# The low parts of an ordinary weight block, made by one subtraction into two places of a ring of five

## The chip, the cores and the metric

The kernel runs on one core of one Trainium2 chip. The metric is device time in microseconds (us) of one launch. Of the kernel before there are three runs and one profiled execution with its trace.

## What is computed

The reference is a decoder trunk of two layers over 256 tokens of width 2048, all float32. Layer 0 mixes tokens by retention, layer 1 by a short gated convolution; each is followed by a SwiGLU feed-forward network (FFN). Cut to what carries the time:

```python
for i in range(2):
    mod = c_act @ w_mod[i] + b_mod[i]; sh1, sc1, g1, sh2, sc2, g2 = split(mod, 6)
    h = rms_norm(x, norm1_g[i]) * (1 + sc1) + sh1
    y = retention_mixer(h, ...) if i == 0 else short_conv_mixer(h, ...)   # h @ w_in ... @ w_out
    x = x + g1 * y
    h = rms_norm(x, norm2_g[i]) * (1 + sc2) + sh2
    a, b = split(h @ ffn_w_in[i], 2)
    x = x + g2 * ((silu(a) * b) @ ffn_w_out[i])
return rms_norm(x, final_g)
```

## The kernel before, in words

**High and low parts.** A float32 product is made of faster matmuls on values of type float32r. Each factor is split: the high part is the value cast to float32r (ScalarE), the low part is the value less its high part (VectorE). A product then takes three terms: high by high, high by low, low by high.

**The stream of weights.** All weights of the trunk's products stand in one array `w_all`, in blocks of 128 x 2048 (1 MB), in the order of use. A block lands in one of four `raw` buffers (`fetch`, L378). `prepare` (L393) then makes a piece of it ready: a cast on ScalarE (L419, named hi) and a subtraction on VectorE (L422, named lo). The parts go to a ring of `PLACES` = 5 places of 1024 columns each, one ring for the high and one for the low parts (L426). The list `pieces` (L376) says which pieces a block is cut into:

- an ordinary block is two pieces, (0, 1): its left and its right half, each with one cast and one subtraction of 1024 columns and one place;
- a block of class `Seven` (L134) serves a product of 2 x 2 blocks in seven multiplications instead of eight. It is four pieces, (2, 3, 4, 5): VectorE makes differences of the block's parts (L406, L410, L412), and the pieces take three places of 1024 columns and one place that holds only 512.

A piece numbered 6, a whole block into two places at once, is known to `prepare` and to `fits` (L431) but stands in no list of the kernel before.

**What sets the order.** TensorE's instructions run in the order in which the program is written. `take` (L434) hands the next weight columns to a matmul. When a place is used up, it is dropped, and behind the opening `take` calls `prepare` as long as `fits` allows: one place must be free for a piece, two for piece 6. So a place is written anew when TensorE has done with it, and TensorE comes to it again after the four other places. Behind the opening the instructions of VectorE and ScalarE are put in order by a scheduler, not by hand; each engine then runs its own list strictly in order. In the opening (the retention mixer's first input products) they stand in written order, and only one to three pieces are made ahead.

**How long a place lasts.** In `product` (L462: retention and convolution) a place of 1024 columns serves eight pairs of matmuls, of 512 and of 256 columns (L472, L475). In `by_token` (L492: the FFNs) an ordinary place serves twelve matmuls of 512 columns through `thrice` (L482 to L489, the rows of the trace being L485, L486 and L487; L486 is the one that reads the low part of the weights when they stream, and it comes second). A place of a Seven serves six of them (L201, `sevens`), its last place of 512 columns three.

**Which blocks are Sevens.** In each FFN the blocks of a group of columns come in rows of eight to twelve; the numbers of the rows that are Sevens are written down: `FFN_SEVEN` = (2, 4, 6) for the first FFN's input products (ten groups), `IN_SEVEN` = (3, 4, 6) for the last FFN's (ten groups), and `OUT_SEVEN` for its output products.

**Beside it on VectorE:** 192 modulation sums over blocks of 2048 columns (L326 and, in the opening, L798), sums and splits of results, and the mixers' own arithmetic.

Of the kernel before, what the change touches and what calls it, by code (L numbers as in the profile page):

```python
# [10 lines left out]
F32 = mybir.dt.float32  # L11
F32R = mybir.dt.float32r
I32 = mybir.dt.int32
AF = mybir.ActivationFunctionType
ALU = mybir.AluOpType
PSUM = bass.MemoryType.PSUM

P = 128
# [13 lines left out]
CHUNK = 2048  # L32
HALF = 1024
# [20 lines left out]
PLACES = 5  # L54
FETCHED, PLAIN, WARM, ADDED = 2, 3, (5, 0, 0, 0, 0, 0, 0, 8), ()
# [23 lines left out]
def ret_in_groups():  # L79

    qkg, v = [], []
    for h in range(HEADS):
        q = [Q0 + h * DK + i * P for i in range(2)]
        k = [K0 + h * DK + i * P for i in range(2)]
        qkg.append([q, k, [(G0 + h * DV, DV)]])
        v.append(Group([V0 + h * DV], DV))
    done = [0] * HEADS  # L90
    spans = []
    for heads, (a, b) in SPANS:
        assert all(done[h] == a for h in heads)
        for h in heads:
            done[h] = b
        spans.append(Group([c for h in heads for part in qkg[h] for c in part], ks=range(a, b)))
    rest = [[Group(c, ks=range(done[h], KT)) for c in qkg[h]] for h in range(HEADS)]
    return spans, list(zip(rest, v))
# [28 lines left out]
RET_SPANS, RET_HEADS = ret_in_groups()  # L127
# [6 lines left out]
class Seven:  # L134
# [6 lines left out]
    n = 2 * DV // P  # L141
# [123 lines left out]
def trunk(ctx: ExitStack, tc: tile.TileContext, x_in, c_in, pos_in, w_mod, cols_in, gain_in, tab_in, w_all, out):  # L265
    nc = tc.nc
    const = ctx.enter_context(tc.tile_pool(name="const", bufs=1))
    work = ctx.enter_context(tc.tile_pool(name="work", bufs=2))
    wpool = ctx.enter_context(tc.tile_pool(name="wpool", bufs=1))
# [8 lines left out]
    def tmp(tag, shape=(P, S), dtype=F32, pool=work, bufs=None):  # L278
        return pool.tile(list(shape), dtype, tag=tag, name=name(tag), bufs=bufs)
# [12 lines left out]
    at = [0]  # L292
# [76 lines left out]
    ready, place, raws, fetched, n_fetched = [], [None], [], {}, [0]  # L369
    in_seven, n = set(), 0  # L370
# [2 lines left out]
            in_seven.add(n // CHUNK)  # L373
        n += g.n * P * len(g.ks)

    pieces = [(i, p) for i in range(PLAIN, w_all.shape[0]) for p in ((2, 3, 4, 5) if i in in_seven else (0, 1))]  # L376

    def fetch():  # L378
        raw = wpool.tile([P, CHUNK], F32, tag="raw", name=name("raw"), bufs=RAW_BUFS)
        nc.sync.dma_start(raw, w_all[n_fetched[0]])  # L380
        fetched[n_fetched[0]] = raw
        n_fetched[0] += 1
# [3 lines left out]
    def next_raw(i=None):  # L386
        i = used[0] if i is None else i
        used[0] += i < PLAIN
        while n_fetched[0] <= i + (FETCHED if i < PLAIN else 0):
            fetch()  # L390
        return fetched.pop(i)

    def prepare(between=None):  # L393
        if prepared[0] == len(pieces):
            return
        index, piece = pieces[prepared[0]]
        prepared[0] += 1
        if piece in (0, 2, 6):
            raws[:] = [next_raw(index)]
            while first <= units[0] < early and len(fetched) < RAW_BUFS - 1 and n_fetched[0] < w_all.shape[0]:  # L400
                fetch()
        whole = raws[0]
        b = [whole[:, i : i + DV] for i in range(0, CHUNK, DV)]
        raw = whole[:, :HALF] if piece in (0, 4) else whole[:, HALF:] if piece < 6 else whole
        if piece == 2:
            nc.vector.tensor_tensor(differences[0], whole[:, DV : 3 * DV], whole[:, : 2 * DV], op=ALU.subtract)  # L406
        elif piece == 3:
            raw = differences[0]
        elif piece == 4:
            nc.vector.tensor_tensor(b[1], b[2], differences[0][:, :DV], op=ALU.subtract)  # L410
        elif piece == 5:
            nc.vector.tensor_tensor(b[3], b[3], b[1], op=ALU.subtract)  # L412
            raw = b[3]
        width, at = raw.shape[1], HALF * (taken_places[0] % PLACES)
        taken_places[0] += -(-width // HALF)
        hi, lo = [t[:, at : at + width] for t in split_weights]
        steps = [slice(i, min(i + HALF, width)) for i in range(0, width, HALF)]
        for o in steps:
            nc.scalar.copy(hi[:, o], raw[:, o])  # L419
        if between:  # L420
            between()
        nc.vector.tensor_tensor(lo, raw, hi.bitcast(F32), op=ALU.subtract)  # L422
        ready.extend((hi[:, o], lo[:, o], o.stop - o.start) for o in steps)

    taken_places = [0]
    split_weights = [  # L426
        wpool.tile([P, PLACES * HALF], F32R, tag=tag, name=tag) for tag in ("hi", "lo")
    ]
    prepared = [0]

# [3 lines left out]
    def take(group, k, col, width=P):  # L434

        assert order.pop() == (group, k, col, width)
        i = place[0] or 0
        if i == 0:
            if place[0] == 0:
                ready.pop(0)  # L440
            while len(ready) < 1 + AHEAD * (units[0] >= first) or units[0] >= early and fits():
                n = len(ready)
                prepare()
                if len(ready) == n:
                    break
        place[0] = (i + width) % ready[0][2]
        return [t[:, i : i + width] for t in ready[0][:2]]
# [274 lines left out]
    with ExitStack() as inner:  # L722
# [64 lines left out]
        with tc.tile_pool(name="start", bufs=1) as sp:  # L787
# [59 lines left out]
            with tc.manual_schedule(engines={mybir.EngineType.DVE, mybir.EngineType.Activation}):  # L847
# [92 lines left out]
                def between(k):  # L940
                    lows[k]()
                    both_reduced(k)
                    if k == FIRST_KS - 1 and PLAIN == FIRST_KS:
                        prepare()
                        prepare()
# [10 lines left out]
            due, step = [], [0.0]  # L956
            at, plain_rows = 0.0, range(PLAIN - FIRST_KS)
            if plain_rows:
                due += [(len(plain_rows) - PREPARED + 0.5 * i, prepare) for i in range(2)]
            for k in range(FIRST_KS, KT):  # L960
                steps = ROW_STEPS[(k >= ROWS_AT[0]) + (k >= ROWS_AT[1])]
# [358 lines left out]
    with tc.tile_pool(name="ffn", bufs=1) as fpool:  # L1320
# [5 lines left out]
        for part in range(2):  # L1326
            n = FFN_TILES[part] // 2
# [19 lines left out]
    for i, g in enumerate(CONV_IN):  # L1347
        pending += [sums(g)] if i else normed(acc, 1, 0, g)
        while len(pending) >= 3:
# [3 lines left out]
            b, c, u = pb(tmp("bsum", pool=mpool, bufs=2)), pc(), pu()  # L1353
# [149 lines left out]
    for part in range(2):  # L1503
        n = LAST_TILES[part] // 2
# [54 lines left out]
```

## Time and profile before

| | before |
|---|---|
| three runs, median (lowest, highest) | 2562.66 us (2562.12, 2562.8) |
| the profiled execution's span, first to last instruction | 2558.4 us, 4.3 us less than the median run |
| TensorE (PE) busy | 2539.3 us, 99% |
| VectorE (DVE) busy | 2354.7 us, 92% |
| ScalarE (ACT) busy | 1351.2 us, 53% |
| DMA, mean | 269 GB/s |

The profiled execution has no time of its own beside its span; what lies around the span is taken as the 4.3 us. In the rows a start is in us from the span's start, and after it comes the duration; "x3" is three instructions in a row merged into one. PE is a matmul, PEld its weight load. A matmul's end is modelled, and matmuls overlap, so the distance of two starts says how long TensorE really takes for one.

### The profile page before, as it was taken

How to read it: one execution, taken by the hardware profiler on the slowest of the kernel's cores; microseconds unless marked ns; L12 is line 12 of the kernel's file. 1: busy time of each engine (PE TensorE's matmuls, PEld its weight loads, DVE VectorE, ACT ScalarE, POOL GpSimd, SP SyncE). 2: the span in 40 equal slices, each digit the busy share in tenths (PEclk: the TensorE clock that was granted, in tenths of full speed). 3: DMA queues.
4: the chain of work that ended last, by engine and by line, in shares of the span. 5: the costliest groups of instructions: out<-in, count | busy, mean ns of one | idle time of the engine just before them, and what ended most of it. 6: DMA issues, size and time to landing. Idle time of an engine off the chain costs nothing.

```text
span 2558.4 us, 34761 instructions
## 1 busy us (share of the span) xinstructions
PE 2539.3 (99%) x13237; PEld 2181.4 (85%) x13237; DVE 2354.7 (92%) x2968; ACT 1351.2 (53%) x1799; POOL 179.3 (7%) x234
## 2 busy tenths in 40 slices
PE   8999999999999999999999999999999999999998
PEld 7898888888889888888888898888998888888886
DVE  7989999898899999889999899888989999999998
ACT  5544543454456554345555454445566555555554
POOL 0000121011110001000000012000000000000001
PEclk9999999999999999999999999999999999999999
DMA  9987888879875667866667879888846465555653
GB/s 399 396 329 264 319 317 340 333 287 331 325 281 213 237 234 293 336 249 228 216 228 299 328 270 344 314 306 309 323 158 215 180 230 214 181 214 183 228 183 146
DMA packets 96695, 689.47 MB, mean 269 GB/s; under 512 B 10744, under 2 KB 12168, under 8 KB 13456
## 3 DMA queue, kind: packets, MB, share of 16 engines
q1 hardware_dynamic: 96528, 687.25, 72.2%
q8 instruction: 103, 1.69, 0.3%
q14 instruction: 64, 0.52, 0.1%
HBM read 685.11 MB, written 2.11 MB: 269 GB/s over the span
## 4 chain that ended last, share of the span: by engine, by line
PE 94%; DVE 3%; DMA 1%; ACT 1%; issue 1%; POOL 0%; SPq 0%; ACTq 0%; POOLq 0%; DVEq 0%
PE bank L472 22%; PE bank L487 17%; PE bank L485 17%; PE bank L486 17%; PE bank L475 11%; DVE lo L422 1%; PE bank L667 1%; PE bank L669 1%; PE bank L668 1%; PE bank L536 1%; PE bank L535 1%; PE bank L534 1%; DVE raw L798 1%; DMA raw<-w_all 1%; PE bank L1290 1%; PE bank L1067 1%
## 5 line engine op out<-in xcount | busy, mean ns | idle before, releaser
L419 ACT CAST hi<-raw 128x1024 fp32r<-128x1024 f32 (+1 forms) x984 | 991.1, 1019 | 936.7 <-PE bank L487 325.1
L422 DVE TENSOR_TENSOR lo<-raw,hi 128x1024 fp32r<-128x1024 f32 (+1 forms) x984 | 1143.3, 1179 | 125.6 <-ACT hi L419 116.7
L485 PE MATMUL bank<-hi,h 128*128 128x512 f32 x1540 | 602.9, 391 | 0.0
L487 PE MATMUL bank<-hi,h 128*128 128x512 f32 x1540 | 601.2, 390 | 0.0
L486 PE MATMUL bank<-lo,h 128*128 128x512 f32 x1540 | 601.1, 390 | 0.0
L326 DVE SCALAR_TENSOR_TENSOR raw<-raw,cb 128x2048 f32<-128x2048 f32 x160 | 365.4, 2285 | 8.2 <-DMA raw<-w_mod 8.0
L472 PE MATMUL bank<-h,hi 128*128 128x512 f32 x1012 | 352.8, 392 | 0.0
L487 PEld LDWEIGHTS bank<-hi,h 128*128 128x128 f32 x1540 | 289.4, 188 | 61.0
L485 PEld LDWEIGHTS bank<-hi,h 128*128 128x128 f32 x1540 | 289.6, 188 | 58.1
L486 PEld LDWEIGHTS bank<-lo,h 128*128 128x128 f32 x1540 | 289.7, 188 | 57.5
L472 PE MATMUL bank<-mid,hi 128*128 128x512 f32 x920 | 319.4, 391 | 0.0
L475 PE MATMUL bank<-h,lo 128*128 128x256 f32 x1012 | 285.0, 282 | 0.0
L475 PE MATMUL bank<-mid,lo 128*128 128x256 f32 x920 | 259.7, 282 | 0.0
L472 PEld LDWEIGHTS bank<-h,hi 128*128 128x128 f32 x1012 | 190.1, 188 | 40.3
L472 PEld LDWEIGHTS bank<-mid,hi 128*128 128x128 f32 x920 | 172.9, 188 | 35.6
L475 PEld LDWEIGHTS bank<-h,lo 128*128 128x128 f32 x1012 | 191.6, 189 | 0.5
L475 PEld LDWEIGHTS bank<-mid,lo 128*128 128x128 f32 x920 | 174.3, 189 | 0.1
L472 PE MATMUL bank<-rm,hi 128*128 128x512 f32 x496 | 172.5, 391 | 0.0
L475 PE MATMUL bank<-rm,lo 128*128 128x256 f32 x496 | 140.0, 282 | 0.0
L487 PE MATMUL bank<-hi,mid 128*128 128x512 f32 x284 | 110.9, 391 | 0.0
L485 PE MATMUL bank<-hi,mid 128*128 128x512 f32 x284 | 110.9, 391 | 0.0
L486 PE MATMUL bank<-lo,mid 128*128 128x512 f32 x284 | 110.7, 390 | 0.0
(300 smaller groups left out, 3344.2 us busy)
## 6 DMA issues: line engine op xcount, KB each, us to landing
raw<-w_all SPq DMA_DIRECT2D x456, 1024.0 KB, 5.0
raw<-w_mod SPq DMA_DIRECT2D x192, 1024.0 KB, 6.1
x<-x_in SPq DMA_DIRECT2D x4, 512.0 KB, 5.3
out<-xt SPq DMA_DIRECT2D x4, 512.0 KB, 3.0
decay<-tab_in SPq DMA_DIRECT2D x8, 128.0 KB, 4.9
x<-gate_row SPq DMA_DIRECT2D x2, 512.0 KB, 4.6
last_gain<-gain_in SPq DMA_DIRECT2D x1, 1024.0 KB
cols<-cols_in SPq DMA_DIRECT2D x1, 152.0 KB, 8.2
```

The source lines that it names most:

```text
L326: nc.vector.scalar_tensor_tensor(raw, raw, 1.0, cb, op0=ALU.mult, op1=ALU.mult, accum_out=total)
L419: nc.scalar.copy(hi[:, o], raw[:, o])
L422: nc.vector.tensor_tensor(lo, raw, hi.bitcast(F32), op=ALU.subtract)
L472: nc.tensor.matmul(pt, hi, h, start=fresh and k == g.ks[0], stop=False, skip_group_check=True)
L475: nc.tensor.matmul(pt[:, 1, :], lo, h[:, 0, :], start=False, stop=last and k == g.ks[-1], skip_group_check=True)
L485: nc.tensor.matmul(o, hi, w_hi, start=first, stop=False)
L486: nc.tensor.matmul(o, hi, w_lo, start=False, stop=False)
L487: nc.tensor.matmul(o, lo, w_hi, start=False, stop=last)
L534: nc.tensor.matmul(pt, hi, h[:, 0, :], start=first, stop=False, skip_group_check=True)
L535: nc.tensor.matmul(pt, hi, h[:, 1, :], start=False, stop=False, skip_group_check=True)
L536: nc.tensor.matmul(pt, lo, h[:, 0, :], start=False, stop=last, skip_group_check=True)
L667: nc.tensor.matmul(pt, hi, high, start=k == 0, stop=False, skip_group_check=True)
```

## The change

An ordinary block behind the opening (`apart` lists the blocks of the opening) becomes one piece, number 6. Its two casts stay two instructions of 1024 columns; its two subtractions become one of 2048 columns, which writes two places of the ring at once. The ring tile gets a dimension for the place, so that the two places may also be the last and the first (a step of -4 places). Since piece 6 needs two free places, `take` asks for an ordinary block when the second of two places has been used up. Blocks of the opening and Sevens keep their pieces.

```diff
-    pieces = [(i, p) for i in range(PLAIN, w_all.shape[0]) for p in ((2, 3, 4, 5) if i in in_seven else (0, 1))]
+    apart = range(sum(g.n * len(g.ks) for g in RET_SPANS) * P // CHUNK + 1)
+    pieces = [(i, p) for i in range(PLAIN, w_all.shape[0]) for p in ((2, 3, 4, 5) if i in in_seven else (0, 1) if i in apart else (6,))]
...
-        width, at = raw.shape[1], HALF * (taken_places[0] % PLACES)
-        taken_places[0] += -(-width // HALF)
-        hi, lo = [t[:, at : at + width] for t in split_weights]
-        steps = [slice(i, min(i + HALF, width)) for i in range(0, width, HALF)]
-        for o in steps:
-            nc.scalar.copy(hi[:, o], raw[:, o])
+        width, at = raw.shape[1], taken_places[0] % PLACES
+        n = -(-width // HALF)
+        taken_places[0] += n
+        rows = [raw[:, i : min(i + HALF, width)] for i in range(0, width, HALF)]
+        his, los = [[t[:, (at + i) % PLACES, : v.shape[1]] for i, v in enumerate(rows)] for t in split_weights]
+        for hi, v in zip(his, rows):
+            nc.scalar.copy(hi, v)
         if between:
             between()
-        nc.vector.tensor_tensor(lo, raw, hi.bitcast(F32), op=ALU.subtract)
-        ready.extend((hi[:, o], lo[:, o], o.stop - o.start) for o in steps)
+        if n == 1:
+            nc.vector.tensor_tensor(los[0], raw, his[0].bitcast(F32), op=ALU.subtract)
+        else:
+            step = 1 if at + 1 < PLACES else 1 - PLACES
+            end = None if at + 2 * step < 0 else at + 2 * step
+            hi, lo = [t[:, at:end:step, :] for t in split_weights]
+            raw = raw.rearrange("p (a b) -> p a b", a=2)
+            nc.vector.tensor_tensor(lo, raw, hi.bitcast(F32), op=ALU.subtract)
+        ready.extend((hi, lo, v.shape[1]) for hi, lo, v in zip(his, los, rows))
...
-        wpool.tile([P, PLACES * HALF], F32R, tag=tag, name=tag) for tag in ("hi", "lo")
+        wpool.tile([P, PLACES, HALF], F32R, tag=tag, name=tag) for tag in ("hi", "lo")
```

Behind the opening 346 blocks become such pairs. Two places on VectorE show how its list changes. The first is in the last FFN. Here x8 is the tile of a Seven's differences, raw_2116 is a block of a Seven and raw_2115 the ordinary block used before it; the row that makes raw_2115's low parts comes behind the low parts of the Seven ahead of both (raw_2114, whose piece of 512 columns is the first row shown). Before:

```order
L422 TENSOR_TENSOR lo_94<-raw_2114_18769,hi_93 128x512
L406 TENSOR_TENSOR x8_75<-raw_2116_18821 128x1024
L422 TENSOR_TENSOR lo_94<-raw_2115_18803,hi_93 128x1024 x2
L422 TENSOR_TENSOR lo_94<-raw_2116_18821,hi_93 128x1024
L422 TENSOR_TENSOR lo_94<-x8_75,hi_93 128x1024
L410 TENSOR_TENSOR raw_2116_18821<-raw_2116_18821,x8_75 128x512
```

And now, with the rows of raw_2114 from its first low part on:

```order
L425 TENSOR_TENSOR lo_94<-raw_2114_18460,hi_93 128x1024
L413 TENSOR_TENSOR raw_2114_18460<-raw_2114_18460 128x512
L425 TENSOR_TENSOR lo_94<-x8_75,hi_93 128x1024
L425 TENSOR_TENSOR lo_94<-raw_2114_18460,hi_93 128x1024
L425 TENSOR_TENSOR lo_94<-raw_2114_18460,hi_93 128x512
L407 TENSOR_TENSOR x8_75<-raw_2116_18511 128x1024
L411 TENSOR_TENSOR raw_2116_18511<-raw_2116_18511,x8_75 128x512
L431 TENSOR_TENSOR lo_94<-raw_2115_18500,hi_93 128x2048
L425 TENSOR_TENSOR lo_94<-raw_2116_18511,hi_93 128x1024
```

The two subtractions of raw_2115 have become one, and one more of the next Seven's differences (L411, before L410) now stands ahead of it.

The second place is in the convolution, where every block is ordinary. L326 is a modulation sum; sum, cu and y are tiles of the mixer. Before:

```order
L422 TENSOR_TENSOR lo_94<-raw_1608_13847,hi_93 128x1024
L326 SCALAR_TENSOR_TENSOR raw_1621_13939,msum_1622_13941<-raw_1621_13939,cb_71 128x2048
L546 TENSOR_TENSOR sum_1616_13900<-bank_1607_13846,low_1615_13898 128x256
L422 TENSOR_TENSOR lo_94<-raw_1620_13913,hi_93 128x1024
L1356 TENSOR_TENSOR cu_1617_13902<-sum_1614_13896,sum_1616_13900 128x256
L422 TENSOR_TENSOR lo_94<-raw_1620_13913,hi_93 128x1024
```

And now:

```order
L431 TENSOR_TENSOR lo_94<-raw_1610_13642,hi_93 128x2048
L326 SCALAR_TENSOR_TENSOR raw_1621_13711,msum_1622_13713<-raw_1621_13711,cb_71 128x2048
L555 TENSOR_TENSOR sum_1616_13673<-bank_1607_13620,low_1615_13671 128x256
L1365 TENSOR_TENSOR cu_1617_13675<-sum_1614_13669,sum_1616_13673 128x256
L431 TENSOR_TENSOR lo_94<-raw_1620_13702,hi_93 128x2048
```

The two halves of raw_1620 stood on both sides of the mixer's cu and are now one instruction behind it. TensorE's list has the same matmuls in the same order as before.

## The prediction

> **What bounds the kernel now.** I read the page's busy shares first, then the windows by stage, then the waits of TensorE behind the opening.
>
> ```profile
> span 2558.4 us, 34761 instructions
> PE 2539.3 (99%) x13237; PEld 2181.4 (85%) x13237; DVE 2354.7 (92%) x2968; ACT 1351.2 (53%) x1799; POOL 179.3 (7%) x234
> ```
>
> ```profile
> core 0: us, PE busy (x) PEld busy (x) DVE busy (x) ACT busy (x) POOL busy (x), PEclk, DMA share, GB/s
> 192.00:832.00 640.00, 639.46 (x3449) 554.55 (x3448) 590.09 (x802) 315.44 (x466) 83.27 (x109) 1.00 0.81 301
> 832.00:1360.00 528.00, 528.00 (x2514) 443.25 (x2513) 493.43 (x548) 279.42 (x306) 30.57 (x33) 1.00 0.69 253
> 1910.00:2558.00 648.00, 638.88 (x2854) 528.75 (x2852) 609.95 (x742) 372.59 (x445) 9.62 (x10) 1.00 0.55 197
> ```
>
> ```profile
> engine line waited for: us in total, times, longest us
> PE bank L1067 <- DVE sp L552: 0.5, 1, 0.5
> ```
>
> The last answer is that of TensorE's waits from 192 us, where the opening ends, up to 2540 us: one wait of 0.5 us. In the first FFN (832 to 1360) PE is busy without a gap, at the full clock. VectorE, though busy 93% there and 94% in the last FFN (1910 to 2558), holds nobody up. A share of 99% alone would not prove it, since a matmul's record overlaps the next one's; the starts do:
>
> ```profile
> 2234.01 0.39 PE L487 MATMUL bank<-hi,h 128*128 128x512 f32 x1
> 2234.24 0.39 PE L485 MATMUL bank<-hi,sum 128*128 128x512 f32 x1
> 2234.47 0.39 PE L486 MATMUL bank<-lo,sum 128*128 128x512 f32 x1
> ...
> 2237.64 0.39 PE L485 MATMUL bank<-hi,h 128*128 128x512 f32 x1
> 2237.87 0.39 PE L486 MATMUL bank<-lo,h 128*128 128x512 f32 x1
> ```
>
> From 2234.01 to 2237.87 there are 17 steps, 0.227 us each, the same 0.23 between neighbours: no gap. [...] So a gain on VectorE has next to nothing to shorten, and the question is whether the new form makes TensorE wait.
>
> **What is removed: 346 subtractions' starts.** The rows are the groups of VectorE by shape.
>
> ```profile
> L422 DVE TENSOR_TENSOR lo<-raw,hi 128x1024 fp32r<-128x1024 f32 x906 | 1096.0, 1221 | 124.8 <-ACT hi L419 115.9 <-PE bank L472 2.5
> L326 DVE SCALAR_TENSOR_TENSOR raw<-raw,cb 128x2048 f32<-128x2048 f32 x160 | 365.4, 2285 | 8.2 <-DMA raw<-w_mod 8.0
> ```
>
> A subtraction of 2048 isn't in the trace. One of 1024 takes 1.22; the nearest row with 2048 columns is the modulation sum, 2.29. I take 2.29 (upper end 2 x 1.22 = 2.44). Back to back, three of 1024 take 3.49 (row at 2235.32 below), that is (3.49 - 1.22) / 2 = 1.14 for each further one. A pair now takes 1.14 + 1.22 = 2.36, so 0.07 is saved, 346 times: 24 us of VectorE's time. As TensorE waits for VectorE behind the opening 0.5 us in all, I put that at 0. [...]
>
> **What is added: the first place of a pair waits for its second.** Before, the low part of the first half could be made as soon as its own place was free and cast. Now it must wait until TensorE has left the second place too, the second cast is done, and the double subtraction has run whole. Behind it on VectorE stand the next low parts and differences, and TensorE waits for it. When the second place comes free, TensorE has the three other places left to work on. How long these last decides.
>
> *Pairs among ordinary blocks.* In the convolution a place comes free at the end of the first row's matmul, and the pair that is then prepared is wanted by the second row:
>
> ```profile
> 1649.12 0.28 PE L475 MATMUL bank<-h,lo 128*128 128x256 f32 x1
> ...
> 1657.78 0.28 PE L475 MATMUL bank<-h,lo 128*128 128x256 f32 x1
> ```
>
> 1657.78 - 1649.40 = 8.38 us. The work to be done in it is 3.6 (below), so 4.8 is left, enough for two modulation sums of 2.29 in the way. I put these at 0. If that cover went, each would cost what its queue exceeds 4.8 by.
>
> *Pairs behind a Seven.* Here the three places are those of a Seven, 6 + 6 + 3 = 15 matmuls of 0.227, 3.4 us. By the written lists there are 30 in the first FFN (ten groups, rows 3, 5, 7) and 37 in the last (20 behind `IN_SEVEN`, rows 5 and 7 of ten groups; 17 in the outputs): 67. Take the place whose order is shown above. Its second place is left by the matmul at 2234.01, which ends at 2234.40; its low part is wanted at 2237.87: 3.47 us. Now the steps, from ScalarE and VectorE around there:
>
> ```profile
> 2228.36 1.05 ACT L419 CAST hi<-raw 128x1024 fp32r<-128x1024 f32 x1 [3.48 <-PE bank L487]
> 2229.72 1.05 ACT L419 CAST hi<-x 128x1024 fp32r<-128x1024 f32 x1 [0.31 <-PE bank L487]
> 2231.08 1.58 ACT L419 CAST hi<-raw 128x1024 fp32r<-128x1024 f32 x2 [0.31 <-PE bank L487]
> 2234.49 1.06 ACT L419 CAST hi<-raw 128x1024 fp32r<-128x1024 f32 x1 [0.31 <-PE bank L487]
> ...
> 2244.70 1.05 ACT L419 CAST hi<-raw 128x1024 fp32r<-128x1024 f32 x1 [0.32 <-PE bank L487]
> ```
>
> ```profile
> 2229.45 1.22 DVE L422 TENSOR_TENSOR lo<-raw,hi 128x1024 fp32r<-128x1024 f32 x1 [2.25 <-ACT hi L419]
> 2230.71 0.69 DVE L412 TENSOR_TENSOR raw<-raw 128x512 f32<-128x512 f32 x1
> 2231.32 1.22 DVE L422 TENSOR_TENSOR lo<-x,hi 128x1024 fp32r<-128x1024 f32 x1
> 2235.32 3.49 DVE L422 TENSOR_TENSOR lo<-raw,hi 128x1024 fp32r<-128x1024 f32 x3
> ...
> 2244.41 3.95 DVE L422 TENSOR_TENSOR lo<-raw,hi 128x1024 fp32r<-128x1024 f32 x3 [0.84 <-ACT hi L419]
> ```
>
> The second cast starts at 2234.49, 0.09 behind the release, and ends at 2235.55. VectorE starts 0.04 behind a cast (2228.36 + 1.05 = 2229.41, then 2229.45): 2235.59 if it is free. Plus 2.29: 2237.88. What a late low part costs TensorE is seen once in the opening:
>
> ```profile
> 54.30 1.22 DVE L422 TENSOR_TENSOR lo<-raw,hi 128x1024 fp32r<-128x1024 f32 x1
> ```
>
> ```profile
> 55.02 0.28 PE L535 MATMUL bank<-h,hi 128*128 128x256 f32 x1
> 55.58 0.39 PE L536 MATMUL bank<-h,lo 128*128 128x256 f32 x1 [0.27 <-DVE lo L422]
> 55.80 0.28 PE L534 MATMUL bank<-h,hi 128*128 128x256 f32 x1
> 55.92 0.28 PE L535 MATMUL bank<-h,hi 128*128 128x256 f32 x1
> ```
>
> The matmul starts 0.05 behind the subtraction's end (55.52), and the next one follows after 0.22 instead of 0.12, since its own weight load no longer ran ahead: 0.15 in all. So the least loss at this place is 2237.88 + 0.15 - 2237.87 = 0.16 us.
>
> Is VectorE free at 2235.59? In the new order, from 2229.45: low part 1.14, L413 0.61 (2230.71 to 2231.32), two low parts 2 x 1.14, one of 512 at 0.61, the differences L407 1.14 and L411 0.61: 2235.84. All their casts are done by then (the last, of two in the row at 2231.08, at 2232.66). So the pair ends at 2238.13 and the loss is 0.41. At the next tight place VectorE has nothing left in the way: the cast ends at 2245.75 and the pair at 2248.08, against
>
> ```profile
> 2244.21 0.39 PE L487 MATMUL bank<-hi,h 128*128 128x512 f32 x1
> ...
> 2248.07 0.39 PE L486 MATMUL bank<-lo,h 128*128 128x512 f32 x1
> ```
>
> which is a loss of 0.16. The mean of the two is 0.285; for 37 places 10.5 us. In the first FFN a tight place is a little wider:
>
> ```profile
> 968.63 0.40 PE L487 MATMUL bank<-hi,h 128*128 128x512 f32 x1
> ...
> 972.58 0.39 PE L486 MATMUL bank<-lo,h 128*128 128x512 f32 x1
> ```
>
> 3.55 instead of 3.47, so I take 0.04 less on average, 0.25; for 30 places 7.5 us. **Sum: 18 us**, on the span 2558.4 + 18 = 2576.4, and with the 4.3 us around it, which I leave as they are, 2580.7.
>
> **Bounds of that term.** From below: VectorE free at all 67 places and the wider lead everywhere, 0.16 - 0.08 = 0.08 each, 5 us. From above: VectorE gets to the pair only when, in the trace of before, it got to the second half. At the first place that is 2235.32 + 1.14 = 2236.46, a loss of 1.03 by the same sum; at the second the pair's second half is the middle one of the three at 2244.41, which can start at its cast's end, 2245.79, as above: 0.16. Mean 0.6, 67 times: 40 us, 2602.7.
>
> **Other edits.** The casts keep number, size and engine; ScalarE has 47% free. The pair may start in place 4 and end in place 0: the same columns, no more instructions. The block's load is issued from the same queue in the order of use, a place later in the program; a raw buffer is given back at most one subtraction (1.14) later. Between these bounds (0 and a delay of 1.14 against the 4.8 left in loose places) I take 0.
>
> **Rivals.**
> 1. *Nothing moves.* The tight places hold: the double subtraction ends before 2237.72, so takes under 2.13 instead of 2.29, or the release comes earlier than modelled. For it: the losses are tenths of a us on a lead of 3.5. Against it: the cast starts 0.09 behind the modelled end, and 2048 columns took 2.29. Time 2562.7; chance 0.08.
> 2. *Faster.* VectorE is the real bound in the FFNs, and 24 us less work on it shows. It decides if TensorE's steps were longer than a matmul needs; at 0.227 for 512 columns over the whole FFN, and with 0.5 us of waits, there is nothing to take it from. The full 24 us would give 2538.7. Chance 0.05. [...]
> 3. *Much slower.* VectorE, idle for 648 - 610 = 38 us in the last FFN, must now stand still for each second cast in order, and the work behind (evictions, differences) comes late in turn: each tight place costs 1.03, as the worst above, 67 x 1.03 = 69 us, 2632. It decides when VectorE's forced stand exceeds that idle time, 1 us for each of 37 places. Against it: at the two places worked out nothing is late behind the pair. Chance 0.08.
>
> **The numbers.** The forecast, 5 to 40 us slower, has 0.79. Its range is 2567.7 to 2602.7; I give 2568 to 2603, which leaves out most of the three rivals. About 0.2% (5 us) is what a measurement of this kernel can tell from no change. Faster by more: 0.05. Within: 0.08, and nearly nothing of the forecast's lower end. Slower by more: 0.87.
>
> **What would show it.** Right: PE waits for the L431 subtraction some 67 times, 0.1 to 0.5 us each, all between 830 and 1360 or behind 1910 us, none in the convolution (1360 to 1910); the group of 2048 columns has 346 instructions near 2290 ns; VectorE's busy sum falls by about 24 us. Wrong: no such waits, or waits in the convolution and retention too, or waits of more than 1 us.

## The result, and the profile after

The changed kernel takes 2588.0 us (median of four runs, 2586.84 to 2588.81); the kernel before, four runs beside it, 2562.39. The ratio is 1.0102, with a 95% interval of 1.0088 to 1.0117: 25.6 us slower, where 18 were forecast. It lies in the range.

**The page.** Its head, and the row of the double subtractions from the list by shape:

```profile
span 2587.0 us, 34323 instructions
PE 2555.6 (99%) x13237; PEld 2174.9 (84%) x13237; DVE 2329.3 (90%) x2622; ACT 1351.5 (52%) x1799; POOL 187.9 (7%) x234
L431 DVE TENSOR_TENSOR lo<-raw,hi 128x2048 fp32r<-128x2048 f32 x346 | 791.3, 2288 | 138.8 <-ACT hi L421 136.5
```

VectorE's busy time fell by 25.4 us (2354.7 to 2329.3), as 346 pairs at 0.07 should give, and the span grew by 28.6. This is more than the 25.6 between the medians because of the span of before. In every listed run the time is 1.7 to 1.9 us more than the span, so 2558.4 belongs to an execution of some 2560.2, quicker than the median one.

The last row also shows what took the saving's place: in front of the double subtractions VectorE now stood still for 136.5 us, waiting for ScalarE's cast (L421). Before, the wait for casts in front of the subtractions of 1024 was 115.9. Over all low parts it was 117.1 before and is 167.9 now.

**The waits.** First of TensorE's weight loads before, then the four longest sums now, then those of its matmuls for the double subtraction, from 192 us on (up to 2560 before, to 2570 now); the columns are the sum in us, the number and the longest:

```profile
PEld bank L1067 <- DVE sp L552: 0.9, 1, 0.9
PEld bank L1067 <- ACT sp L551: 0.2, 1, 0.2
```

```profile
PEld bank L495 <- DVE lo L431: 28.5, 67, 1.5
PEld bank L495 <- DVE lo L425: 4.6, 3, 1.9
PEld bank L1076 <- ACT sp L560: 1.6, 1, 1.6
PEld bank L494 <- DVE u L1233: 1.0, 1, 1.0
```

```profile
PE bank L495 <- DVE lo L431: 6.5, 14, 1.0
```

Where the loads waited twice before, 67 waits stand for the double subtraction alone. L495 is the matmul that reads the low part (L486 before); the retention mixer runs it too, 412 times between 192 and 832 us, and waits there nowhere. That they are 67 is in part chance: 66 stand at tight places and one, at 2567 us, at a loose pair of the last outputs. The 67th tight place, the first of the first FFN, has no wait of its own, because TensorE was held up 1.77 us three matmuls ahead of it.

Neither sum is the time lost: a weight load normally starts ahead of its matmul (0.22 us in the median of those at L494 to L496) and so has some time to wait for nothing, and a matmul's modelled record, 0.39 us where the next one starts 0.23 behind it, hides short gaps. The loss is read from the starts. TensorE's 13,237 matmuls have the same order in both kernels, so the distance from each start to the next can be set against the same distance before. What is added by this at the 67 tight places, and at the matmul behind each, is 16.8 us: 4.7 in the first FFN, 12.1 in the last. The median is 0.17, 16 places lose over 0.3, and the most is 1.18. The same sum over everything behind the opening gives 2.8 in the retention (192 to 832 of before), 8.4 in the first FFN, 0.9 in the convolution, 16.9 in the last FFN: 29.0.

So 12.2 us come from elsewhere, and ten of them from seven places: 2.8 near 230 us, where TensorE waits for the retention's scores; 1.77 at 838.5, 1.2 at 2064 and 1.2 at 2151, for a Seven's own low part (L425), which at 838.5 stands behind a double one in VectorE's list; 0.85 at 912 for a sum of products (u); 0.9 at 1509 for a norm's result (rs); and 1.3 at the loose pair at 2567.

**The worked place.** The pair that the prediction followed at 2234 us of before stands at 2257.70 now. VectorE, then TensorE:

```profile
2251.10 1.22 DVE L425 TENSOR_TENSOR lo<-raw,hi 128x1024 fp32r<-128x1024 f32 x1 [1.47 <-ACT hi L421]
2252.36 0.69 DVE L413 TENSOR_TENSOR raw<-raw 128x512 f32<-128x512 f32 x1
2252.97 1.22 DVE L425 TENSOR_TENSOR lo<-x,hi 128x1024 fp32r<-128x1024 f32 x1
2254.11 1.82 DVE L425 TENSOR_TENSOR lo<-raw,hi 128x1024 fp32r<-128x1024 f32 x2
2255.84 1.22 DVE L407 TENSOR_TENSOR x<-raw 128x1024 f32<-128x1024 f32 x1
2257.10 0.69 DVE L411 TENSOR_TENSOR raw<-raw,x 128x512 f32<-128x512 f32 x1
2257.70 2.28 DVE L431 TENSOR_TENSOR lo<-raw,hi 128x2048 fp32r<-128x2048 f32 x1
```

```profile
2259.30 0.39 PE L494 MATMUL bank<-hi,h 128*128 128x512 f32 x1
2260.04 0.50 PE L495 MATMUL bank<-lo,h 128*128 128x512 f32 x1 [0.36 <-DVE lo L431]
2260.38 0.40 PE L496 MATMUL bank<-hi,h 128*128 128x512 f32 x1
2260.62 0.39 PE L494 MATMUL bank<-hi,h 128*128 128x512 f32 x1
```

The pair starts 6.60 behind the first row, not the 6.39 worked out; it ends at 2259.98 and the matmul starts 0.06 later. That step is 0.74 instead of 0.227 and the next 0.34: a loss of 0.51 + 0.11 = 0.63, not 0.41. The missing 0.2 is in the list: where an instruction writes what the one ahead of it reads, or reads what that one writes (L425 then L413, L407 then L411), the starts of these rows lie 1.26 apart, and 1.14 where they have nothing to do with each other (2252.97, then 2254.11).

**The stages.** The windows of after, in the columns of the prediction's:

```profile
192.00:832.00 640.00, 638.12 (x3436) 553.02 (x3435) 579.23 (x692) 313.67 (x463) 86.50 (x109) 1.00 0.81 301
832.00:1367.00 535.00, 532.03 (x2501) 438.84 (x2500) 486.56 (x476) 277.75 (x305) 32.41 (x33) 1.00 0.67 247
1920.00:2587.00 667.00, 650.47 (x2865) 527.30 (x2863) 605.84 (x672) 373.95 (x447) 6.90 (x10) 1.00 0.54 192
```

The first FFN's PE was busy 528.00 of 528; now 532.03 of 535 at the same full clock. The gaps are real waits, and VectorE is further from busy than before (487 of 535 us, where it was 493 of 528): it is late, not full.

### The profile page after: what moved, and what is told of

Same layout as the page of the kernel before. It is cut to its first block, busy times and chain, and to the rows that moved or that the text cites. A ratio compares the mean times of both kernels' runs of the same rounds, so it can differ in the third digit from the quotient of the medians.

```text
span 2587.0 us, 34323 instructions
## 1 busy us (share of the span) xinstructions
PE 2555.6 (99%) x13237; PEld 2174.9 (84%) x13237; DVE 2329.3 (90%) x2622; ACT 1351.5 (52%) x1799; POOL 187.9 (7%) x234
## 4 chain that ended last, share of the span: by engine, by line
PE 86%; DVE 9%; DMA 2%; issue 2%; ACT 1%; POOL 0%; ACTq 0%; POOLq 0%; SPq 0%; DVEq 0%
PE bank L481 21%; PE bank L495 15%; PE bank L496 15%; PE bank L494 15%; PE bank L484 11%; DVE lo L431 2%; DVE lo L425 2%; DMA raw<-w_mod 1%; PE bank L676 1%; PE bank L678 1%; PE bank L677 1%; PE bank L545 1%; PE bank L544 1%; ACT hi L421 1%; PE bank L543 1%
## 5 line engine op out<-in xcount | busy, mean ns | idle before, releaser
L421 ACT CAST hi<-raw 128x1024 fp32r<-128x1024 f32 (+1 forms) x984 | 991.2, 1018 | 930.2 <-PE bank L496 306.0
L431 DVE TENSOR_TENSOR lo<-raw,hi 128x2048 fp32r<-128x2048 f32 x346 | 791.3, 2288 | 138.8 <-ACT hi L421 136.5
L495 PE MATMUL bank<-lo,h 128*128 128x512 f32 x1540 | 605.9, 393 | 6.4 <-DVE lo L431 3.7
L494 PE MATMUL bank<-hi,h 128*128 128x512 f32 x1540 | 602.6, 391 | 0.6 <-DVE u L1233 0.6
L496 PE MATMUL bank<-hi,h 128*128 128x512 f32 x1540 | 600.8, 390 | 0.0
L326 DVE SCALAR_TENSOR_TENSOR raw<-raw,cb 128x2048 f32<-128x2048 f32 x160 | 365.3, 2284 | 4.0 <-DMA raw<-w_mod 3.9
L495 PEld LDWEIGHTS bank<-lo,h 128*128 128x128 f32 x1540 | 289.3, 188 | 79.2 <-DVE lo L431 19.7
L494 PEld LDWEIGHTS bank<-hi,h 128*128 128x128 f32 x1540 | 289.3, 188 | 60.0 <-DVE u L1233 1.0
L425 DVE TENSOR_TENSOR lo<-raw,hi 128x1024 fp32r<-128x1024 f32 (+1 forms) x292 | 310.4, 1078 | 32.4 <-ACT hi L421 31.1
L496 PEld LDWEIGHTS bank<-hi,h 128*128 128x128 f32 x1540 | 289.2, 188 | 59.8
L495 PE MATMUL bank<-lo,mid 128*128 128x512 f32 x284 | 112.7, 397 | 3.8 <-DVE lo L431 2.7
L496 PE MATMUL bank<-hi,mid 128*128 128x512 f32 x284 | 111.0, 391 | 0.0
```

What stands on the lines that cost most here:

```text
L326: nc.vector.scalar_tensor_tensor(raw, raw, 1.0, cb, op0=ALU.mult, op1=ALU.mult, accum_out=total)
L421: nc.scalar.copy(hi, v)
L425: nc.vector.tensor_tensor(los[0], raw, his[0].bitcast(F32), op=ALU.subtract)
L494: nc.tensor.matmul(o, hi, w_hi, start=first, stop=False)
L495: nc.tensor.matmul(o, hi, w_lo, start=False, stop=False)
L496: nc.tensor.matmul(o, lo, w_hi, start=False, stop=last)
```

## The experiments

The recorded expectations name these theories. **A**: the loss arises at the 67 tight places and is the chain (cast, subtraction, weight load) less the lead, plus VectorE's queue. **B**: a longer instruction delays VectorE's list everywhere, in proportion to the number of pairs. **C**: it is the asking for two places at once. **D**: it is the waiting of the first half for the second place and cast, whatever the length of the subtraction. **E**, formed on the way: single places where the new order of VectorE's list puts something long ahead of something urgent. "Behind the opening" means the sum over the starts; the opening itself differed by 0 to 2.3 us between runs of kernels that are alike there (all but the two with six places, whose opening is told with them). In each, `pieces` or `prepare` of the changed kernel is edited, in run 6 two of its constants, and in run 7 the same two of the kernel before; of a changed line only the part that differs is shown.

**1. Only loose pairs** (279 of 346 by the trace, where the expectation says 276; the ordinary blocks behind a Seven keep two pieces):

```
- (0, 1) if i in apart else (6,)
+ (0, 1) if i in apart or i - 1 in in_seven else (6,)
```

> The change, but an ordinary block that stands right behind a Seven keeps its two pieces and two subtractions; 276 of the 346 pairs remain, none with a lead of 3.5 us. Theory A (the loss sits at the 67 tight places, where the chain of second cast and double subtraction is longer than the lead): 2563 to 2570 us; what is left over are the few late places that are not tight (in the trace after: 2.8 us in the retention mixer, 0.9 at the start of the convolution, some 4 in single places). Theory B (a long instruction in VectorE's list makes others late everywhere, in proportion to the number of pairs): 25.6 x 276 / 346 = 20 us, so about 2583.

Measured: 2573.94 us against 2562.05, 1.0046 (1.0029 to 1.0063), +11.9. The tight places lose nothing; the 13.0 behind the opening are spread: retention 2.8, first FFN 4.3, convolution 1.8, last FFN 4.2. The waits of the weight loads, from 192 to 2560 us:

```profile
PEld bank L494 <- DVE mid L1304: 3.2, 7, 0.7
PEld bank L494 <- DVE extra L1231: 2.4, 5, 0.5
PEld bank L495 <- DVE lo L425: 2.3, 3, 1.0
PEld bank L495 <- DVE lo L431: 1.9, 1, 1.9
```

TensorE waits some twenty times, mostly not for a double subtraction: for sums of the Sevens' products (extra) and low parts of activations (mid) that VectorE reached late. B misses by more than A (it wanted 2583 for four fifths of the pairs, A at most 2570), but that loose pairs cost next to nothing, as A has it, is refuted too: they cost 12 us by themselves.

**2. Only tight pairs** (67):

```
- (0, 1) if i in apart else (6,)
+ (6,) if i not in apart and i - 1 in in_seven else (0, 1)
```

> The opposite: only the 67 blocks right behind a Seven become pairs, all others keep two pieces. Theory A: the loss at the tight places stays, 18.6 us by the trace after, so 2578 to 2584 us. Theory B: 25.6 x 67 / 346 = 5 us, so about 2567.

Measured: 2586.39 us, 1.0096 (1.0081 to 1.0111), +24.3. A fifth of the pairs costs nearly as much as all of them, so B falls; A's band ended at 2584. Behind the opening it is 25.0: 19.9 at the tight places, 5.1 elsewhere in the FFNs, and 0.0 in retention and convolution, where this kernel has no pair.

```profile
PEld bank L495 <- DVE lo L431: 30.1, 66, 1.4
```

Runs 1 and 2 together cost 36, more than the change's 26: the places outside the tight ones (13.0 and 5.1 here, 12.2 there) belong to each kernel's own list and don't add up.

**3. Two places asked for at once, but two subtractions:**

```
- nc.vector.tensor_tensor(lo, raw, hi.bitcast(F32), op=ALU.subtract)
+ for lo, v, hi in zip(los, rows, his):
+     nc.vector.tensor_tensor(lo, v, hi.bitcast(F32), op=ALU.subtract)
```

> The change with its claim of two places at once, but with two subtractions of 1024 columns, each into its own place and waiting for its own cast alone. Theory A: the first low part no longer waits for the second place; no chain is longer than its lead: 2562 to 2566 us. Theory C (the loss comes from asking for two places at once, so from the later place in the program at which a block is prepared): 2585 to 2590, as the change.

Measured: 2560.74 us against 2562.05, 1.0000 (0.9991 to 1.0009); behind the opening no stage changes by more than 0.05. C falls. The shape of the ring, the order of claims and the block's load, all kept here, cost nothing. The raw buffer's later return is not among them, since the second subtraction ends as early here as before. The casts wait for loads 109.6 us in all before, 123.4 here, 135.1 in the change and 185.7 in run 4; whether that costs TensorE anything was not tried.

**4. The same work cut the other way**, two subtractions that each write half of both places, so both wait for both casts, but half of the result is there 1.07 earlier (2.29 less 1.22):

```
- nc.vector.tensor_tensor(lo, raw, hi.bitcast(F32), op=ALU.subtract)
+ for o in (slice(0, DV), slice(DV, HALF)):
+     nc.vector.tensor_tensor(lo[:, :, o], raw[:, :, o], hi[:, :, o].bitcast(F32), op=ALU.subtract)
```

> The change with two subtractions of 1024 columns, each taking 512 columns of both places, so that both wait for the second cast, but the first is done 1.07 us earlier and holds the columns that TensorE wants first. Theory A: the chain at a tight place is 0.09 + 1.06 + 0.04 + 1.22 + 0.15 = 2.56 us against a lead of 3.47 to 3.55: no loss there but for a queue on VectorE over 0.9 us; 2563 to 2571. Theory D (that the pair must wait for its second place and cast at all is what costs, whatever the length of the subtraction): 2580 to 2590.

Measured: 2574.88 us, 1.0052 (1.0035 to 1.0068), +12.8, between the two. The tight places fall from 16.8 to 2.2, so there it is the length of the subtraction, not the waiting; the other 11.0 are spread like run 1's (retention 1.6, first FFN 5.4, convolution 2.3, last FFN 3.9, less those 2.2).

**5. The cast doubled too**, one of 2048 columns instead of two:

```
- for hi, v in zip(his, rows):
-     nc.scalar.copy(hi, v)
...
+     nc.scalar.copy(split_weights[0][:, at:end:step, :], raw.rearrange("p (a b) -> p a b", a=2))
```

> The change with the two casts of a pair made one of 2048 columns on ScalarE, which can start only when the second place is free. Back to back a further 1024 columns cost about 0.95 us there, so the chain at a tight place grows from 3.6 to 4.55 us against the same lead of 3.5. Theory A (loss at a tight place is chain less lead, plus any queue): 67 x 0.95 = 63 us more than the change, so 2640 to 2660 us. Theory B (what counts is VectorE's list): VectorE does exactly the same and ScalarE less, so no more than the change, about 2588.

Measured: 2673.07 us against 2560.44, 1.0439 (1.0421 to 1.0456), +112.6, which is above A's band. The group of casts, and one tight place on ScalarE, VectorE and TensorE:

```profile
L425 ACT CAST hi<-raw 128x2048 fp32r<-128x2048 f32 x346 | 662.2, 1914 | 698.4 <-PE bank L485 257.0 <-PE bank L500 247.4 <-issue 155.4
```

```profile
2327.97 1.92 ACT L425 CAST hi<-raw 128x2048 fp32r<-128x2048 f32 x1 [1.83 <-issue]
```

```profile
2329.93 2.29 DVE L435 TENSOR_TENSOR lo<-raw,hi 128x2048 fp32r<-128x2048 f32 x1 [0.34 <-ACT hi L425]
```

```profile
2332.27 0.50 PE L499 MATMUL bank<-lo,h 128*128 128x512 f32 x1 [0.75 <-DVE lo L435]
```

The chain is there link by link: cast, 0.04, subtraction, 0.05, matmul. It is longer by 1.91 - 1.05 = 0.86, and the median tight place loses 1.02 instead of 0.17, 0.85 more. Together the tight places lose 75.7. At 75.7 - 16.8 = 58.9 that is the part that A's sum holds (63 expected); the other 39 of the 114 behind the opening were not costed. Some 14 of them are TensorE's clock, which stood at 0.50 for ten stretches of 3.4 us (last section); the rest stands at places off the sum, a norm's h at L624 and the gate's product at L1294 among them.

**6. Six places, three raw buffers** (a sixth place takes the room of a raw buffer), which gives each pair another place's lead:

```
- RAW_BUFS = 4
- PLACES = 5
+ RAW_BUFS = 3
+ PLACES = 6
```

> The change with six places instead of five, paid for with three raw buffers instead of four. A pair behind a Seven then has one more place of work ahead of it, 6 or 3 more matmuls of 0.227, so its lead grows from 3.5 to at least 4.2 us, mostly 4.8, over a chain of 3.6. Theory A: the loss at the tight places goes; 2562 to 2570 us, if three raw buffers keep the loads on time. Theory B: nothing changes on VectorE's list but the time of asking, so about 2580 to 2588; fewer raw buffers could only add to it.

Measured: 2586.98 us, 1.0102 (1.0087 to 1.0117): no gain in the sum, a miss. By stage it is another kernel: the opening loses 5.0, the retention 10.7 instead of 2.8, the two FFNs 4.7 and 6.1 instead of 8.4 and 16.9, and the tight places 3.4 instead of 16.8.

**7. Its control**, the kernel before with the same two numbers:

> Control for six places and three raw buffers: the kernel before with these two numbers, no pairs. If the third raw buffer's absence is what cost time in the opening and the retention mixer of that run (5.0 and 10.7 us by its trace), this kernel loses some 10 to 16 us there too, 2571 to 2577, and nothing in the FFNs. If the pairs did it (theory B), it is at 2560 to 2563.

Measured: 2577.91 us, 1.0060 (1.0046 to 1.0073), +15.7 with no pair in it: 3.1 in the opening, 10.5 in the retention, 1.8 in the convolution, 1.7 in the FFNs. So run 6's loss in the retention comes with the two numbers and not with the pairs; that the casts waited for loads 405 us in all, instead of 110, points at the raw buffer. Its gain at the tight places fits the longer lead.

**8. Tight pairs alone, cut as in run 4:**

> Only the 67 blocks behind a Seven become pairs, and their subtraction is two of 1024 columns, each of 512 columns of both places: both wait for the second cast as in the kernel with the 67 double subtractions (2586), but the first is done 1.07 us earlier. Theory A: chain 2.56 against 3.5, so nearly all of those 24 us go: 2562 to 2567. Theory D (waiting for the second place costs by itself): 2580 or more.

Measured: 2567.69 us against 2560.44, 1.0028 (1.0017 to 1.0039), +7.3 (A wanted at most 2567), where run 2 had +24.3 with one subtraction. The tight places lose 0.6. What is left, some 6 us, is in the FFNs, and TensorE waits for the pieces of the Sevens:

```profile
PEld bank L496 <- DVE lo L425: 6.6, 11, 1.4
PEld bank L496 <- DVE lo L432: 1.7, 5, 0.6
```

D falls with this run and run 4: the first half still waits for the second place and cast, and the tight places are nearly free.

**9. Pairs only outside the FFNs** (160 by the trace), with `in_ffn` the set of the FFNs' blocks:

```
- (0, 1) if i in apart else (6,)
+ (0, 1) if i in apart or i in in_ffn else (6,)
```

> Pairs only in the retention mixer behind the opening and in the convolution; blocks that hold columns of an FFN keep two pieces. No tight place. Theory E (the loss that is left without tight places is that of single places where VectorE's list now puts a long instruction ahead of something urgent): 2.8 us in the retention mixer near 230 us and 0.9 at the start of the convolution, so 2565 to 2567 and no loss in the FFNs. Theory B (in proportion to pairs, 159 of 346): 12 us, 2574.

Measured: 2563.66 us against 2560.44, 1.0012 (1.0003 to 1.0022), +3.2. Behind the opening everything is as before but for 2.8 us at one place, near 230 us; the 0.9 expected at the start of the convolution did not come. VectorE's list there, first of the kernel before, then of this one (sp are the retention's scores):

```profile
228.75 1.23 DVE L422 TENSOR_TENSOR lo<-raw,hi 128x1024 fp32r<-128x1024 f32 x1
229.88 0.63 DVE L552 TENSOR_TENSOR sp<-sum,sp 128x256 fp32r<-128x256 f32 x2
```

```profile
229.27 2.28 DVE L326 SCALAR_TENSOR_TENSOR raw<-raw,cb 128x2048 f32<-128x2048 f32 x1
...
231.48 0.62 DVE L563 TENSOR_TENSOR sp<-sum,sp 128x256 fp32r<-128x256 f32 x2
```

Where a low part of 1.14 stood ahead of the scores, a modulation sum of 2.2 stands now, because the low part waits for its other half in a pair further down (at 232.02). VectorE's part of the scores comes 1.6 later. ScalarE's list has turned there too, before and then now: its cast of the scores stands behind a cast of weights instead of ahead of it.

```profile
228.67 0.61 ACT L551 CAST sp<-sum 128x256 fp32r<-128x256 f32 x2 [1.59 <-DVE sum L1048]
229.18 1.05 ACT L419 CAST hi<-raw 128x1024 fp32r<-128x1024 f32 x1
```

```profile
229.32 1.04 ACT L423 CAST hi<-raw 128x1024 fp32r<-128x1024 f32 x1 [1.98 <-PE bank L546]
230.27 0.60 ACT L562 CAST sp<-sum 128x256 fp32r<-128x256 f32 x2
```

TensorE waits for ScalarE's part first (1.4) and then for VectorE's (0.5, as before). VectorE's comes last and sets the first loss of 1.34; ScalarE's alone would have cost some 0.8, an estimate from the first two matmuls' starts (0.34 apart). The rest of the 2.8 is the clock (last section).

**10. As run 9, with the first six blocks behind the opening left in two pieces:**

```
- apart = range(sum(g.n * len(g.ks) for g in RET_SPANS) * P // CHUNK + 1)
+ apart = range(sum(g.n * len(g.ks) for g in RET_SPANS) * P // CHUNK + 7)
```

> The kernel with pairs in the two mixers only, but the first six blocks behind the opening keep two pieces. By the order of instructions a low part of 1024 columns then stands again where a modulation sum of 2048 had come ahead of the split of the scores (near 230 us). Theory E (single places in VectorE's list): the 2.8 us at that place go, 2560 to 2562 us, no difference from before. Theory B (in proportion to pairs, 153 of 159 left): as before this edit, some 3 us slower than before.

Measured: 2562.42 us against 2562.2, 1.0005 (0.9996 to 1.0014). The place near 230 is as before, in both lists, which shows that its loss came from the order there. But the same order turns up on VectorE at the scores of a later head, and TensorE loses 1.1 at 308.8 us:

```profile
306.10 2.28 DVE L326 SCALAR_TENSOR_TENSOR raw<-raw,cb 128x2048 f32<-128x2048 f32 x1
...
308.31 0.62 DVE L563 TENSOR_TENSOR sp<-sum,sp 128x256 fp32r<-128x256 f32 x2
```

For the mixers E is shown. For the FFNs, runs 1, 4 and 8 show losses away from the tight places, 8.5, 7.1 and 6.1; that each of them is such a displacement was read from who waits for whom and not tried one by one. It stays open which of them would go with which move.

None of these beats the kernel before. Runs 3 and 10 equal it, and with waits of 0.5 us behind the opening there is little that VectorE could give it.

## Why the prediction was right, and where its sum was off

- **What bounds the kernel** held. VectorE was relieved of 25.4 us (24 forecast) and nothing came of it: no stage behind the opening is shorter than before. The rival in which VectorE's time is worth its price is refuted by that.
- **The tight places** held in mechanism, and nearly in size: 18 forecast, 16.8 measured. All 67 waits for L431 are at L495 and in the two FFNs, 66 of them at tight places. The floor of 0.16 at a place is the measured median of 0.17. The queue's share came out lopsided: 0.16 a place in the first FFN (0.25 forecast), which is hardly more than the floor, and 0.33 in the last (0.285). That these two errors offset each other is luck. At the worked place the queue was 0.2 longer, because the prediction took 1.14 for all neighbours although its own row of 2229.45 has the next start 1.26 behind.
- **"No waits of more than 1 us"** failed at single places: a weight load waited for L431 for 1.3 us at a tight place and 1.5 at the loose one, and the greatest loss is the 1.77 above. With a mean of 0.25 that is far from the rival "much slower", which needed 1.03 at each.
- **The term that was mis-sized is "other edits, and loose pairs: 0".** They cost 12.2 us behind the opening, nearly three quarters of what the tight places cost. The lead in the convolution does cover the pair itself, as worked out. What the step left out is that the lists of VectorE and ScalarE are put in order anew ("the casts keep number, size and engine", but not their order), and that things other than weights (scores, evictions, results between layers, the Sevens' own pieces) stand in them with less in hand than 4.8 us. Run 1 measures this by itself at 13.0, run 9 for the mixers at 2.8. The range, 5 to 40 us, was drawn for the tight places alone; that the total lies in it too is due to its width.
- **The 4.3 us around the span** is 1.8 in the runs. As it was used on both sides, the forecast of the difference does not hang on it.

## What to carry to other kernels

Merging two instructions that fill two places of a ring saves little where neighbours already overlap (0.07 us here: 1.14 + 1.22 against 2.29) and moves the first half's result later (1.07 us here, 2.29 less 1.22, besides the wait for the second place and cast); before merging, set the chain from release to use against the lead at the narrowest place of the ring, not the mean one. Where a scheduler orders the list, cost the new order too: an edit that "only" merges can put 2.2 us ahead of what another engine waits for. And a saving on an engine can give no more than the waits for it, 0.5 us here, even at 92% busy.

## What the runs showed of the hardware

**The clock fell behind waits of 1.4 and 0.5 us.** Near 230 us of the changed kernel TensorE waits twice:

```profile
230.84 0.73 PE L1076 MATMUL bank<-v,sp 128*128 128x512 f32 x2 [1.38 <-ACT sp L560]
232.07 0.50 PE L1076 MATMUL bank<-v,sp 128*128 128x512 f32 x1 [0.50 <-DVE sp L561]
...
233.11 0.41 PE L544 MATMUL bank<-h,hi 128*128 128x256 f32 x1
233.33 0.41 PE L545 MATMUL bank<-h,lo 128*128 128x256 f32 x1
```

For some 3 us the matmuls of 256 columns then follow each other by 0.21 instead of 0.12, which adds 1.4 us to a first loss of 1.34: half of the 2.8 at this place. Run 9, with the same two waits, shows the same: its clock is 0.60 from 232 to 234 us and 0.54 from 234 to 236. Ahead of the fall PE idled 1.4 and 0.5 us.

What stands ahead of a fall can be read from the records of the granted clock. Each fall between 192 and 2540 us lasts 3.41 us at 0.50, and the falls of one trace begin whole multiples of 3.413 apart: in run 5 those at 232.60, 843.59 and 1021.08 lie 179 and then 52 of them apart. So the stretches to look at are those of this grid. Three of the changed kernel, then two of run 5 (the second figure is the time that PE was busy, the one after POOL's the granted clock):

```profile
229.15:232.57 3.42, 1.54 (x8) 0.86 (x7) 3.42 (x7) 1.55 (x3) 0.31 (x1) 1.00 0.74 297
232.57:235.98 3.41, 3.41 (x18) 3.41 (x18) 2.77 (x3) 0.69 (x2) 0.00 (x0) 0.50 0.92 312
836.72:840.14 3.42, 1.92 (x9) 1.35 (x8) 3.42 (x4) 1.05 (x1) 0.00 (x0) 1.00 0.34 77
```

```profile
1188.33:1191.74 3.41, 1.33 (x7) 0.80 (x5) 3.41 (x4) 2.47 (x3) 2.17 (x1) 1.00 0.33 79
1191.74:1195.16 3.42, 3.42 (x8) 2.71 (x9) 3.42 (x4) 0.00 (x0) 0.00 (x0) 0.50 1.01 417
```

The twelve traces have 15 such falls, and in the stretch ahead of each PE was busy for 0.30 to 0.51 of the time. Of the other 8,220 stretches none was busy for less than 0.51; the one at 836.72, with a single wait of 1.5 us, was busy for 0.56 and kept its clock. So in these traces the clock fell behind a stretch in which PE was busy for half or less, though far from idle. The bound is not sharp: outside that range, a stretch of 0.45 at the tail of run 1 had no fall behind it and one of 0.52 in run 2's opening did. Each of run 5's ten falls cost 1.4 to 1.7 us. The openings differ by this too: runs 2 and 3, which came out of theirs 1.7 and 2.3 us later, have a fall at 108 us; of the other kernels with five places none has, and none is over 1.0 later.

**A late weight load cost twice.** At the worked place above the matmul that waits starts 0.06 behind the low part, and the one behind it is late by another 0.11. The weight loads of the two are:

```profile
2260.04 0.19 PEld L495 LDWEIGHTS bank<-lo,h 128*128 128x128 f32 x1 [0.78 <-DVE lo L431]
2260.15 0.19 PEld L496 LDWEIGHTS bank<-hi,h 128*128 128x128 f32 x1
```

The second load starts 0.11 behind the first, and its matmul 0.23 behind it, at 2260.38, as elsewhere. Run 5 shows the same step of 0.34 from the matmul that waited to the next.
